# The gate's second half as a second pair of column blocks with two groups of seven products

## The chip, the cores and the metric

The kernel runs on one core of a Trainium2 chip. The metric is the device time of one execution in microseconds; the times of three runs are given as their median. In the profile PE is TensorE (PEld its weight load), DVE VectorE, ACT ScalarE, POOL GpSimd and SP SyncE, which here only issues transfers.

## The reference

One layer of an encoder on 256 rows of 2048 numbers in float32. The change lies in its last step, the per-layer embedding:

```python
gate = jax.nn.sigmoid(rms_norm(x, ple_norm[i]) @ w_ple_gate[i])   # 2048 x 2048
e = (p[i] @ w_ple_proj[i]) * gate                                 # 256 x 2048
x = x + rms_norm(e, ple_post_norm[i])
```

## The kernel before, in words

**Products.** Every float32 matrix product is made of three: a factor is split into a rounded part (`hi`, a cast on ACT, line 181) and the rest (`lo`, a subtraction on DVE, line 184), and PE sums hi x hi (line 323), lo x hi (324) and hi x lo (328). A weight block is loaded as `raw`, four tiles of 128 x 512 (1024 KB), and split in two halves of 128 x 1024 elements. The split weights stand in `whi`/`wlo` (four buffers), and in a phase with groups of seven also in `shi`/`slo` (three). `raw` has five buffers, two of which hold the rows of x to the end, so that three are left for weights; a load is issued when the reads of the buffer's earlier content are done.

**Rows and columns.** The 256 rows are two row tiles t (0 and 1) of 128. The gate's 2048 columns are four column blocks of 512, n = 0 to 3; its 2048 inner terms are four blocks kb = 0 to 3.

**Groups of seven.** `Seven` works on a pair of column blocks. `chunk(kb)` replaces the eight block products (two row tiles, two column blocks, two halves of kb) by seven, in the manner of Strassen and Winograd. The four weight halves b11, b21 (first column block) and b12, b22 (second) give the sums t1 = b11 + b12, t2 = t1 + b22, t4 = t2 + b21 on DVE (line 511), and a DMA issued by POOL adds b22 onto b12. The seven products, in the order 1, 5, 6, 4, 2, 3, 7 (lines 504, 505, 507), take b11, t1, t2, t4, b21, b22 and the accumulated b12, and each of these is split first. On the other side stand sums of the normed rows: `whole_rows` and `sum_forms` (lines 444, 461 and a split). Each product z has a bank of PSUM: 1, 2, 4 and 5 one `acc` each, 6 and 7 one `aux` together, 3 and 8 the other. There are four `acc` and two `aux`, which are given out again in the order in which they come free. Inner blocks outside a group go through `column(side, kbs)`, plain products into the banks 2, 4 or 3, 8.

**The end of the kernel.** The pair n = 0, 1 has one group (kb = 1); `opened` and `gated` combine the banks into the gates, with sigmoids. Then come the projections of p (two inner tiles, one 512 KB load each) for n = 0 and 1, the gate block n = 2 as plain products (`gemm_block`), its projection, and the last column block n = 3 by `gemm_resident`: its weights are split once and kept, row tile 0 runs through all of them, then its projection, then row tile 1, with its projection in two halves. `ple` multiplies projection and gate (line 1570), squares (1571) and applies the gain (1572). When row tile 0 has all its squares, a root and `add` (line 1637) give its output rows, and SP writes them; row tile 1 follows and ends the kernel.

**The order.** Each engine works through its queue in order. PE's order is that of the code; the order on DVE and ACT is set by a scheduler when the program is built, except that `pin` keeps an instruction in its place. `put_off` and `step` place work between the products.

Of the kernel before, what the change touches and what calls it, by code (L numbers as in the profile page):

```python
# [13 lines left out]
ALU = mybir.AluOpType  # L14
# [19 lines left out]
def layer_kernel(ctx: ExitStack, tc: tile.TileContext, a: dict, shapes: dict, out: bass.AP):  # L34
# [35 lines left out]
    def com(tag):  # L70
        return get(comp, tag, *{"sg": (1024, 1), "h": (1024, 2), "sq": (NB, 1), "mid": (2048, 1)}[tag])
# [10 lines left out]
    def small(n=8):  # L82
        return smp.tile([P, 8], F32, tag="sm", name=uid("sm"))[:, :n]
# [1492 lines left out]
    def sigmoid(sg, t, ps):  # L1576
        return nc.scalar.activation(sg[:, t * NB : (t + 1) * NB], ps, AF.Sigmoid, scale=npl.rs(t))

    def gate_block(ps):
        gate = com("h")  # L1580
        for t in range(TT):
            sigmoid(gate, t, ps[t])
        return gate
# [15 lines left out]
    def crossed(s):  # L1599
        v = g1.rearrange("p (t n) -> p t n", t=TT)  # L1600
# [4 lines left out]
    def gated(s):  # L1605
        for t, (ps, other) in enumerate(((s.bank(2), h0[0]), (s.bank(4), h1[1]))):
            nc.vector.tensor_tensor(out=h0[t], in0=ps, in1=other, op=ALU.add)
            sigmoid(g0, t, h0[t])
        crossed(s)

    with sums_phase("sums3") as sevens:
        forms = {1: sum_forms(sevens, whole_rows(sevens, npl(1)), "h")}
        s = Seven(npl, forms.get, ((wg, 0), (wg, NB)), sevens, sevens)
        s.column(0, (0,))
        s.column(1, (0,))
        s.chunk(1, shared)
        put_off(0, opened, s)
        s.column(0, (2,))
        s.column(1, (2,))
        s.column(0, (3,), True)  # L1620
        put_off(0, gated, s)
        s.column(1, (3,), True)
        nc.vector.tensor_tensor(out=g1, in0=s.banks[3.8], in1=g1, op=ALU.add)
        for t in range(TT):
            sigmoid(g1, t, h1[t])
# [5 lines left out]
    gate = com("h")  # L1631
# [11 lines left out]
    s = small(1)  # L1643
    nc.vector.tensor_reduce(out=s, in_=ss[t], axis=AX.X, op=ALU.add)
    r = rsqrt_mean(s, D, 1)
# [142 lines left out]
```

## Time and profile before

| | |
|---|---|
| median of 3 runs | 1818.25 us (1817.67 to 1818.35) |
| profiled execution, from its first to its last instruction | 1817.3 us |
| PE, busy | 1808.1 us, 99% |
| DVE, busy | 1573.3 us, 87% |
| ACT, busy | 1061.1 us, 58% |
| granted PE clock | 1.000 |

A time of the profiled execution besides its span is not given; the median of the runs lies 0.95 us above the span. Busy time is the time in which an engine executes; on PE the ends of products are modelled. The chain that ended last follows the work back from the last instruction, and names what carried it. Rows of the timeline give start, duration, engine, line, operation, what is written from what, and in brackets how long the engine had stood and for what.

### The profile page before, as it was taken

The page shows a single profiled execution, that of the slowest core. Times are in us where ns is not written, and L with a number is a line of the kernel's source. Part 1 is how long each engine was busy: PE and PEld are TensorE (multiplying, and loading weights), DVE is VectorE, ACT ScalarE, POOL GpSimd, SP SyncE. Part 2 cuts the span into 40 slices and gives each one's busy share as a digit, 9 for nine tenths or more (in the row PEclk, how much of TensorE's full clock was granted, in tenths as well). Part 3 has the DMA queues.
Part 4 walks back from the last instruction along what each step waited for, and adds up shares of the span by engine and source line. Part 5 has one row for each costly group of instructions (what it writes and reads, how often), then busy time and mean ns, then how long its engine had stood idle before and what let it go on. Part 6 is the DMA issues. An engine that isn't in the chain of part 4 may idle for free.

```text
span 1817.3 us, 24219 instructions
## 1 busy us (share of the span) xinstructions
PE 1808.1 (99%) x8918; PEld 1496.5 (82%) x8918; DVE 1573.3 (87%) x1839; ACT 1061.1 (58%) x1240; POOL 106.3 (6%) x162
## 2 busy tenths in 40 slices
PE   9999999999999999999999999999999999999998
PEld 7888888888888888888898888888888888888887
DVE  8978889999998896687567899999999999889875
ACT  7444456556565565465685566555565556566664
POOL 0020100000000001110021000000000010000000
PEclk9999999999999999999999999999999999999999
DMA  8899877787877668675646787888777796766673
GB/s 323 266 288 310 262 222 232 233 261 228 261 252 235 186 221 260 195 254 164 219 133 228 221 298 224 258 256 256 235 231 233 236 282 230 235 207 221 203 243 128
DMA packets 235271, 428.41 MB, mean 236 GB/s; under 512 B 24368, under 2 KB 48336, under 8 KB 234992
## 3 DMA queue, kind: packets, MB, share of 16 engines
q1 hardware_dynamic: 223872, 390.06, 65.1%
q0 software_dynamic: 10560, 35.40, 8.9%
q8 instruction: 70, 1.15, 0.3%
q10 hardware_dynamic: 720, 1.41, 0.2%
q14 instruction: 49, 0.40, 0.1%
HBM read 372.41 MB, written 10.88 MB: 211 GB/s over the span
## 4 chain that ended last, share of the span: by engine, by line
PE 95%; DVE 2%; DMA 1%; issue 1%; ACT 1%; SPq 0%; DVEq 0%; ACTq 0%
PE acc L323 16%; PE acc L324 16%; PE acc L328 16%; PE aux L328 7%; PE aux L323 7%; PE aux L324 7%; PE acc L507 5%; PE acc L504 5%; PE acc L505 5%; PE aux L507 3%; PE aux L504 3%; PE aux L505 3%; DVE wlo L184 1%; PE aux L1210 0%; PE acc L1466 0%
## 5 line engine op out<-in xcount | busy, mean ns | idle before, releaser
L184 DVE TENSOR_TENSOR wlo<-raw,whi 128x1024 fp32r<-128x1024 f32 x480 | 580.4, 1222 | 120.7 <-ACT whi L181 120.2
L181 ACT CAST whi<-raw 128x1024 fp32r<-128x1024 f32 x480 | 497.2, 1050 | 286.4 <-PE acc L324 160.9
L323 PE MATMUL acc<-whi,nhi 128*128 128x512 f32 x908 | 356.5, 393 | 1.3 <-ACT whi L274 0.7
L324 PE MATMUL acc<-whi,nlo 128*128 128x512 f32 x908 | 353.7, 390 | 0.0
L328 PE MATMUL acc<-wlo,nhi 128*128 128x512 f32 x908 | 252.4, 389 | 0.0
L184 DVE TENSOR_TENSOR slo<-raw,shi 128x1024 fp32r<-128x1024 f32 x186 | 226.1, 1216 | 15.2 <-ACT shi L181 14.2
L181 ACT CAST shi<-raw 128x1024 fp32r<-128x1024 f32 x186 | 194.9, 1048 | 59.5 <-DMA raw<-in_ffn_w_down 26.1
L323 PEld LDWEIGHTS acc<-whi,nhi 128*128 128x128 f32 x908 | 170.5, 188 | 38.9 <-ACT whi L274 1.7
L328 PEld LDWEIGHTS acc<-wlo,nhi 128*128 128x128 f32 x908 | 170.4, 188 | 35.8 <-DVE wlo L184 0.4
L324 PEld LDWEIGHTS acc<-whi,nlo 128*128 128x128 f32 x908 | 170.5, 188 | 34.6 <-DVE nlo L275 0.3
L181 ACT CAST whi<-sum 128x1024 fp32r<-128x1024 f32 x79 | 83.2, 1054 | 163.7 <-DVE sum L511 152.8
L181 ACT CAST shi<-sum 128x1024 fp32r<-128x1024 f32 x59 | 62.2, 1054 | 106.8 <-DVE sum L511 98.8
L511 DVE TENSOR_TENSOR sum<-sum,raw 128x1024 f32<-128x1024 f32 x92 | 112.1, 1219 | 1.0
L184 DVE TENSOR_TENSOR wlo<-sum,whi 128x1024 fp32r<-128x1024 f32 x79 | 96.2, 1220 | 5.9 <-ACT whi L181 5.3
L574 POOL DMA_DIRECT2D raw<-raw x44 | 38.1, 866 | 1037.6 <-DVE sum L511 634.6
L323 PE MATMUL aux<-whi,nhi 128*128 128x512 f32 x220 | 85.6, 389 | 0.0
L324 PE MATMUL aux<-whi,nlo 128*128 128x512 f32 x220 | 85.6, 389 | 0.0
L184 DVE TENSOR_TENSOR slo<-sum,shi 128x1024 fp32r<-128x1024 f32 x59 | 72.0, 1220 | 1.1 <-ACT shi L181 0.5
L328 PE MATMUL aux<-wlo,nhi 128*128 128x512 f32 x220 | 67.8, 389 | 0.0
L511 DVE TENSOR_TENSOR sum<-raw,raw 128x1024 f32<-128x1024 f32 x46 | 56.1, 1219 | 13.1 <-DMA raw<-in_ffn_w_up 6.3
L323 PE MATMUL acc<-whi,hhi 128*128 128x512 f32 x156 | 60.7, 389 | 0.0
L324 PE MATMUL acc<-whi,hlo 128*128 128x512 f32 x156 | 60.7, 389 | 0.0
(390 smaller groups left out, 3405.5 us busy)
## 6 DMA issues: line engine op xcount, KB each, us to landing
raw<-in_ffn_w_up SPq DMA_DIRECT2D x88, 1024.0 KB, 6.1
raw<-in_ffn_w_down SPq DMA_DIRECT2D x88, 1024.0 KB, 5.3
raw<-in_ffn_w_gate SPq DMA_DIRECT2D x86, 1024.0 KB, 8.0
raw<-in_w_in SPq DMA_DIRECT2D x32, 1024.0 KB, 5.9
raw<-raw POOLq DMA_DIRECT2D x46, 512.0 KB, 5.6
raw<-in_w_out SPq DMA_DIRECT2D x16, 1024.0 KB, 5.4
raw<-in_w_ple_gate SPq DMA_DIRECT2D x16, 1024.0 KB, 5.8
hT<-mid SPq DMA_DIRECT2D x160, 64.0 KB, 4.8
```

Source lines behind the costliest of these rows:

```text
L181: copy = nc.scalar.copy(hi, src)
L184: rest = nc.vector.tensor_tensor(out=lo, in0=src, in1=hi.bitcast(F32), op=ALU.subtract)
L323: nc.tensor.matmul(ps[t], lhsT=lh, rhs=hi[:, j, cols], start=start and j == 0, stop=False)
L324: nc.tensor.matmul(ps[t], lhsT=ll, rhs=hi[:, j, cols], start=False, stop=False)
L328: nc.tensor.matmul(ps[t], lhsT=lh, rhs=lo[:, j, cols], start=False, stop=stop and j == 1)
L504: nc.tensor.matmul(ps, lhsT=lh[j], rhs=hi[:, j], start=begin and j == 0, stop=False)
L505: nc.tensor.matmul(ps, lhsT=ll[j], rhs=hi[:, j], start=False, stop=False)
L507: nc.tensor.matmul(ps, lhsT=lh[j], rhs=lo[:, j], start=False, stop=z in final and j == 1)
L511: nc.vector.tensor_tensor(out=t, in0=x, in1=y, op=ALU.add)
L574: nc.gpsimd.dma_start(b12, b22, accum_op=ALU.add)
```

## The change

The column blocks n = 2 and 3 become a second `Seven` in the same phase. It begins with `chunk(1)` in new banks, then `column(0, (0, 3))`, then `chunk(2)`; the sum forms of kb = 2 are made on the way (`second_form`, ahead of the last column of the first pair). `opened` and `gated` take the pair as an argument. The projections for n = 0, 1, 2 follow. What the last column block still needs, kb = 0 and 3, is `last`: four split halves that stay resident. `last_gate(t)` adds them into bank 3 or 8, sums with what the pair gave on DVE (line 1647 of the changed kernel) and takes the sigmoid; the projection of n = 3 stays as it was, and row tile 1 follows row tile 0.

```diff
-    g0, g1 = es[2:]
-    h0, h1 = ([g[:, t * NB : (t + 1) * NB] for t in range(TT)] for g in (g0, g1))
+    gates = es[2:]
+    def columns(pair):
+        return ([g[:, t * NB : (t + 1) * NB] for t in range(TT)] for g in gates[2 * pair : 2 * pair + 2])
-    def opened(s):
+    def opened(s, pair):
+        h0, h1 = columns(pair)
         nc.scalar.copy(h0[0], s.bank(1))
         nc.vector.tensor_tensor(out=h1[0], in0=s.bank(6), in1=h0[0], op=ALU.add)          # L1593 after
         nc.vector.tensor_tensor(out=h1[1], in0=s.bank(7), in1=h1[0], op=ALU.add)          # L1594
...
+    def gated(s, pair):
+        h0, h1 = columns(pair)
+        v = gates[2 * pair + 1].rearrange("p (t n) -> p t n", t=TT)
+        nc.vector.tensor_tensor(out=h0[0], in0=s.bank(2), in1=h0[0], op=ALU.add)          # L1599
+        nc.vector.tensor_tensor(out=h0[1], in0=s.bank(4), in1=h1[1], op=ALU.add)          # L1600
+        for t in range(TT):
+            sigmoid(gates[2 * pair], t, h0[t])
         nc.vector.tensor_tensor(                                                          # L1603
             out=v, in0=s.bank(5).unsqueeze(1).to_broadcast([P, TT, NB]), in1=v, op=ALU.subtract
         )
...
         s.column(1, (2,))
+        put_off(0, second_form)
         s.column(0, (3,), True)
...
+        s = Seven(npl, forms.get, ((wg, 2 * NB), (wg, 3 * NB)), sevens, sevens)
+        gates += [com("h"), com("h")]
+        s.chunk(1)
+        s.column(0, (0, 3))
+        s.chunk(2, (*shared, 2, 4))
+        opened(s, 1)
+        gated(s, 1)
     own = ctx.enter_context(phase("own"))
-    proj_block(0, g0)
-    proj_block(1, g1)
-    proj_block(2, gate_block(gemm_block(npl, wg, 2 * NB, KD)))
+    for n in range(ND - 1):
+        proj_block(n, gates[n])
+    gate = gates[n + 1]
     n = ND - 1
-    gate = com("h")
-    gates = gemm_resident(npl, a["w_ple_gate"][0], n * NB, KD, own, KD - 8)
+    last = [(npl(kb), half) for kb in (0, 3) for half in weight_halves(wg, 4 * kb, 4, n * NB, own=own)]
     projs = gemm_resident(lambda k: pT, a["w_ple_proj"][0], n * NB, PD // P, own, PD // P, 2)
+    def last_gate(t):
+        z = (3, 8)[t]
+        for part, half in last:
+            gemm_half({t: s.bank(z)}, (part, half), (t,), s.begin(z), half is last[-1][1])
+        g = gate[:, t * NB : (t + 1) * NB]
+        pin(nc.vector.tensor_tensor(out=g, in0=s.bank(z), in1=g, op=ALU.add))             # L1647
+        pin(sigmoid(gate, t, g))
...
     t = 0
-    sigmoid(gate, t, next(gates))
+    last_gate(t)
     ple(n, t, gate, next(projs))
...
     t = 1
-    pin(sigmoid(gate, t, next(gates)))
+    last_gate(t)
```

The names in the rows below carry the number of the buffer's use: `raw_15295` is one load, `wlo_15298` the rest of its weights, `acc_15237` one use of a bank. DVE around the first projection, before: the sums of the first pair (L1607, L1601, L1623), with rests of the gate block n = 2 between them, and `ple` of the projection.

```order
L184 TENSOR_TENSOR wlo_14985<-raw_14982,whi_14984 128x1024
L184 TENSOR_TENSOR wlo_15013<-raw_15010,whi_15012 128x1024
L1607 TENSOR_TENSOR e_2710_14592<-acc_14618,e_2710_14592 128x512
L1607 TENSOR_TENSOR e_2710_14592<-acc_14625,e_2711_14593 128x512
L1601 TENSOR_TENSOR e_2711_14593<-acc_14735,e_2711_14593 128x1024
L184 TENSOR_TENSOR wlo_15041<-raw_15038,whi_15040 128x1024
L1623 TENSOR_TENSOR e_2711_14593<-aux_14661,e_2711_14593 128x1024
L184 TENSOR_TENSOR wlo_15045<-raw_15038,whi_15044 128x1024
L1570 TENSOR_TENSOR e_2710_14592<-acc_14980,e_2710_14592 128x512
L1570 TENSOR_TENSOR e_2710_14592<-acc_14981,e_2710_14592 128x512
```

DVE at the same place after: `raw_15146` is the second load of the group kb = 2, `raw_15239`, `raw_15267` and `raw_15295` are the weights of the projections n = 0, 1 and 2.

```order
L184 TENSOR_TENSOR wlo_15216<-raw_15146,whi_15215 128x1024
L184 TENSOR_TENSOR wlo_15242<-raw_15239,whi_15241 128x1024
L184 TENSOR_TENSOR wlo_15270<-raw_15267,whi_15269 128x1024
L184 TENSOR_TENSOR wlo_15298<-raw_15295,whi_15297 128x1024
L1593 TENSOR_TENSOR h_14988<-aux_15024,h_14987 128x512
L1570 TENSOR_TENSOR e_2710_14592<-acc_15237,e_2710_14592 128x512
L1594 TENSOR_TENSOR h_14988<-aux_15024,h_14988 128x512
L1599 TENSOR_TENSOR h_14987<-acc_15048,h_14987 128x512
L1600 TENSOR_TENSOR h_14987<-acc_15037,h_14988 128x512
L1572 TENSOR_TENSOR e_2708_14590<-e_2710_14592,pg_14587 128x512
L1603 TENSOR_TENSOR h_14988<-acc_15011,h_14988 128x1024
L1570 TENSOR_TENSOR e_2710_14592<-acc_15238,e_2710_14592 128x512
```

The rests of all three projections have moved ahead of the pair's combining and of the first `ple`. The load of `raw_15295` takes the buffer of `raw_15146`. PE's product into `acc_15238`, the bank of the first projection's second row tile, waits for the first L1570, whose `acc_15237` lies in the same bank; before, the product into `acc_14981` waits for the first L1607.

DVE at the end of row tile 0, before: the four adds of row tile 0, two small operations, and the product of row tile 1's gate and projection.

```order
L1646 TENSOR_SCALAR sm_15317<-sm_15317 128x1
L1637 SCALAR_TENSOR_TENSOR x_12725<-e_2708_14590,sm_15317,x_12725 128x512
L1637 SCALAR_TENSOR_TENSOR x_12725<-e_2709_14591,sm_15317,x_12725 128x512
L1637 SCALAR_TENSOR_TENSOR x_12725<-e_2710_14592,sm_15317,x_12725 128x512
L1637 SCALAR_TENSOR_TENSOR x_12725<-e_2711_14593,sm_15317,x_12725 128x512
L1656 TENSOR_REDUCE sm_15386<-sm_14589 128x1
L1657 TENSOR_SCALAR sm_15386<-sm_15386 128x1
L1666 TENSOR_TENSOR h_15205<-acc_15394,h_15205 128x256
```

After, the same place; L1652 is what was L1637, L1681 what was L1666:

```order
L1661 TENSOR_SCALAR sm_15388<-sm_15388 128x1
L1652 SCALAR_TENSOR_TENSOR x_12725<-e_2708_14590,sm_15388,x_12725 128x512
L1652 SCALAR_TENSOR_TENSOR x_12725<-e_2709_14591,sm_15388,x_12725 128x512
L1652 SCALAR_TENSOR_TENSOR x_12725<-e_2710_14592,sm_15388,x_12725 128x512
L1652 SCALAR_TENSOR_TENSOR x_12725<-e_2711_14593,sm_15388,x_12725 128x512
L1647 TENSOR_TENSOR h_14988<-aux_15059,h_14988 128x512
L1671 TENSOR_REDUCE sm_15433<-sm_14589 128x1
L1672 TENSOR_SCALAR sm_15433<-sm_15433 128x1
L1681 TENSOR_TENSOR h_14988<-acc_15441,h_14988 128x256
```

The addition that completes row tile 1's gate (L1647) is new and stands behind the four adds of row tile 0; before, the sigmoid read PE's bank itself.

More of the change, by code (lines that the diff above doesn't have):

```diff
@@ L1577, in sigmoid @@
         return nc.scalar.activation(sg[:, t * NB : (t + 1) * NB], ps, AF.Sigmoid, scale=npl.rs(t))
-    def gate_block(ps):
-        gate = com("h")
-        for t in range(TT):
-            sigmoid(gate, t, ps[t])
-        return gate
     def proj_block(n, gate):
@@ L1597, in opened @@
         nc.vector.tensor_tensor(out=h1[1], in0=s.bank(7), in1=h1[0], op=ALU.add)
-    def crossed(s):
-        v = g1.rearrange("p (t n) -> p t n", t=TT)
+    def gated(s, pair):
[5 more added lines that the diff above has]
+            sigmoid(gates[2 * pair], t, h0[t])
         nc.vector.tensor_tensor(
@@ L1603, in crossed, with second_form @@
         )
[L1605 to L1609, printed above, removed]
     with sums_phase("sums3") as sevens:
         forms = {1: sum_forms(sevens, whole_rows(sevens, npl(1)), "h")}
+        def second_form():
+            forms[2] = sum_forms(sevens, whole_rows(sevens, npl(2)), "h")
         s = Seven(npl, forms.get, ((wg, 0), (wg, NB)), sevens, sevens)
@@ L1640, in layer_kernel @@
     t = 0
-    sigmoid(gate, t, next(gates))
+    last_gate(t)
     ple(n, t, gate, next(projs))
-    s = small(1)
-    nc.vector.tensor_reduce(out=s, in_=ss[t], axis=AX.X, op=ALU.add)
-    r = rsqrt_mean(s, D, 1)
+    total = small(1)
+    nc.vector.tensor_reduce(out=total, in_=ss[t], axis=AX.X, op=ALU.add)
+    r = rsqrt_mean(total, D, 1)
     nc.vector.tensor_scalar(r, r, -2.0, None, op0=ALU.mult)
```

9 lines of the change are left out of this document (4 added, 5 removed).

## The prediction

> **What bounds the kernel now.** I read the page first: the busy rows and the chain that ended last.
>
> ```profile
> PE 1808.1 (99%) x8918; PEld 1496.5 (82%) x8918; DVE 1573.3 (87%) x1839; ACT 1061.1 (58%) x1240; POOL 106.3 (6%) x162
> ...
> PE 95%; DVE 2%; DMA 1%; issue 1%; ACT 1%; SPq 0%; DVEq 0%; ACTq 0%
> ```
>
> PE carries 95% of the chain, so a product taken away is worth its pitch, as long as the weights are split in time. VectorE (DVE) is second with 87%. Next the stages that change: the busy time by window, then the rows of each engine in order of time.
>
> ```profile
> core 0: us, PE busy (x) PEld busy (x) DVE busy (x) ACT busy (x) POOL busy (x), PEclk, DMA share, GB/s
> 1740.00:1800.00 60.00, 60.00 (x266) 49.60 (x265) 40.25 (x50) 33.86 (x46) 0.00 (x0) 1.00 0.51 173
> ...
> 1753.30 0.39 PE L323 MATMUL acc<-whi,pT 128*128 128x512 f32 x1
> 1753.53 0.39 PE L324 MATMUL acc<-whi,pT 128*128 128x512 f32 x1
> ...
> 1755.28 0.91 PE acc L328 x4
> 1758.00 0.91 PE acc L328 x4
> ```
>
> PE never pauses there, and DVE has 60.00 - 40.25 = 19.75 us free. The two rows of the chain lie twelve products apart: 2.72 us, so 0.2267 us a product. At 1753.30 PE turns from the first pair to the first projection; up to there the change leaves its order alone. I go on from that instant, on the clock of this execution.
>
> **The products.** Two groups of seven replace eight block products each: 12 products fewer, 12 x 0.2267 = 2.72 us.
>
> **What the groups ask of DVE.**
>
> ```profile
> 1726.03 1.22 DVE L184 TENSOR_TENSOR slo<-raw,shi 128x1024 fp32r<-128x1024 f32 x1
> 1727.17 1.22 DVE L184 TENSOR_TENSOR wlo<-raw,whi 128x1024 fp32r<-128x1024 f32 x1
> ...
> 1719.39 1.22 DVE L511 TENSOR_TENSOR sum<-sum,raw 128x1024 f32<-128x1024 f32 x1
> ...
> 1709.60 0.76 DVE L461 TENSOR_TENSOR rows<-whole 128x256 f32<-128x256 f32 x2
> ...
> 1756.00 1.29 DVE L1570 TENSOR_TENSOR e<-acc,e 128x512 f32<-128x512 f32 x2
> 1757.20 1.28 DVE L1572 TENSOR_TENSOR e<-e,pg 128x512 f32<-128x512 f32 x2
> ...
> 1721.65 1.05 ACT L181 CAST whi<-raw 128x1024 fp32r<-128x1024 f32 x1
> 1722.60 1.05 ACT L181 CAST shi<-sum 128x1024 fp32r<-128x1024 f32 x1
> ...
> L574 POOL DMA_DIRECT2D raw<-raw x44 | 38.1, 866 | 1037.6 <-DVE sum L511 634.6
> ```
>
> A 1024-wide rest or sum costs DVE a pitch of 1.14 us, a 512-wide operation 0.60, a 256-wide one 0.36 (between its 0.34 and the 0.38 of half the row), a cast on ScalarE (ACT) 0.95. A group needs 7 rests and 3 sums, 11.4 us, while PE works 42 x 0.2267 = 9.5; the two column blocks that it replaces needed 4 rests, 4.6 us. Twice that is +13.6 us. The sum forms of block 2 (two 1024-wide operations, four of 256) are +3.7; the five combining operations of the second pair +3.5; the last gate's two additions +1.2. That is 22 us more where 19.75 are free: DVE, not PE, becomes the bound, and the order on DVE decides. ACT gets seven casts more, 6.7 us, and is busy for 33.86 of the 60 us, so it covers them; SP issues as many loads as before; POOL issues two accumulating DMAs of 0.87 us each with nothing queued behind them. I cost these three at nothing.
>
> **Where DVE's work meets a load.** A weight load is issued when the last rest has read its buffer.
>
> ```profile
> 1736.82 1.22 DVE L184 TENSOR_TENSOR slo<-raw,shi 128x1024 fp32r<-128x1024 f32 x1
> 1739.49 1.22 DVE L184 TENSOR_TENSOR slo<-raw,shi 128x1024 fp32r<-128x1024 f32 x1
> ...
> 1738.07 0.37 SPq L313 DMA_DIRECT2D raw<-in_w_ple_proj  x1
> 1740.74 0.37 SPq L313 DMA_DIRECT2D raw<-in_w_ple_proj  x1
> ...
> raw<-in_w_ple_gate SPq DMA_DIRECT2D x12, 1024.0 KB, 5.7
> raw<-in_w_ple_proj SPq DMA_DIRECT2D x4, 512.0 KB, 3.8
> ...
> DMA to landing us min/median/max: 3.7/5.3/8.1
> ```
>
> The rest of 1736.82 ends at 1738.04 and the load follows at 1738.07; so too 1740.71 and 1740.74. Weights have three buffers here. The same two instants now issue the two loads of the first group, at 5.7 us for 1024 KB; the second lands at 1746.4. The steps, in DVE's order:
>
> 1. From 1746.8 (the rest of the first block precedes) to the last rest of column block 0's second half: 14 operations of 1024 and 2 of 512, 15.9 + 1.2, with 0.1 of waits: it ends at 1764.1. PE's groups in this stretch have their weights just in time; two of the margins are under 0.4 us. I cost that at nothing, since DVE stays the later one.
> 2. That rest frees the buffer of the second load of group two: issued 1764.1, landed 1769.8.
> 3. Nine operations of 1024 (three sums and the rests of blocks two to seven), 10.2 us and 0.4 of waits for casts: the seventh rest ends at 1780.4. The accumulating DMA, issued from POOL behind the first sum (1771.1), is in by 1776.7 at the 5.6 us of its row below, ahead of its cast at 1777.7.
> 4. That rest frees the buffer of the third projection's weights: 3.8 us, landed 1784.2; cast 1.05; DVE's rest, which stands in its queue ahead of all of the pair's combining, ends its pitch at 1786.5.
> 5. Then L1593 (0.60) and the first L1570 (0.69): 1787.8. Only this L1570 gives back the bank into which PE writes the first projection's second row tile. Without a wait PE would write it at 1753.30 + 138 x 0.2267 + 0.1 = 1784.7: PE stands 3.1 us.
>
> ```profile
> raw<-raw POOLq DMA_DIRECT2D x46, 512.0 KB, 5.6
> ```
>
> 6. From there to the rest of the last projection DVE has 14 operations of 512 and 6 of 1024, 15.2 us, and 0.6 of waits: 1803.5. PE waits for rests of the last gate column twice, 1.1 and 0.4 us. The first row tile's gate ends at 1803.55. Unhindered it would end at 1753.30 + 200.1 x 0.2267 + 0.17 (a product runs on past its pitch) = 1798.84; the waits add 3.1 + 1.1 + 0.4 + 0.1 = 4.7 us.
>
> **The end, row tile by row tile.**
>
> ```profile
> 1793.68 0.61 PE L328 MATMUL acc<-wlo,nhi 128*128 128x512 f32 x2
> ...
> 1794.33 0.69 ACT L1577 ACTIVATE h<-acc,sm 128x512 f32<-128x512 f32 x1 [6.61 <-PE acc L328]
> 1795.76 0.69 DVE L1570 TENSOR_TENSOR h<-acc,h 128x512 f32<-128x512 f32 x1 [6.02 <-PE acc L328]
> 1797.23 1.28 ACT L204 ACT_TABLE_LOAD   x1
> 1799.91 2.74 DVE L1637 SCALAR_TENSOR_TENSOR x<-e,sm,x 128x512 f32<-128x512 f32 x4
> ...
> 1806.57 0.69 ACT L1577 ACTIVATE h<-acc,sm 128x512 f32<-128x512 f32 x1 [6.54 <-PE acc L328]
> 1807.35 0.42 DVE L1666 TENSOR_TENSOR h<-acc,h 128x256 f32<-128x256 f32 x1 [4.45 <-ACT h L1577]
> ```
>
> Before, tile 0's work from L1570 (1795.76) to the end of its four adds (1802.65) takes 6.9 us and lies under the 48 products of tile 1's gate. Now tile 1's gate is 24 products, 5.4 us, and on DVE its addition (L1647) stands behind tile 0's adds. From the end of tile 0's gate: addition 0.73, sigmoid 0.76 (each with its hand-over of 0.04), 6.9 to the end of the adds (the next operation enters 0.05 earlier), addition 0.73, sigmoid 0.76, and 0.1 of hand-overs: 10.0 us to tile 1's product with the projection (L1681, L1666 before). 1803.55 + 10.0 = 1813.56, where before it stood at 1807.35: +6.2 us. Before, the same stretch took 1807.35 - 1794.29 = 13.1 us, of which PE's 24 products and a shorter projection are the saving already counted. What follows has the same instructions, 9.95 us to the span's end of 1817.3.
>
> Sum: -2.7 (products) + 4.7 (waits) + 4.2 (the end: 10.0 without waits would give 1808.85, +1.5 against before, and the 2.7 that PE had saved is lost in it) = +6.2 us. The span becomes 1823.5. The three runs' median, 1818.25, is 0.95 above the profiled span; with that kept, 1824.5.
>
> **The bounds.** Two loads lie on the path (steps 1 and 2), two more of 512 KB follow. With the shortest landing of the rows, 3.7, for all, the loads of 1024 KB give 2 x 2.0 back, but the PE saving limits what is left: no less than the end alone, +1.5. With 8.1 for both, 2 x 2.4 = +4.8. I take the median, the value for twelve such loads in this stretch. Beyond that, 0.2 us for each of the two tight margins of step 1.
>
> The clock:
>
> ```profile
> 1812.00:1815.00 3.00, 0.43 (x2) 0.00 (x0) 0.93 (x2) 0.58 (x1) 0.00 (x0) 1.00 0.87 312
> 1815.00:1817.30 2.30, 0.00 (x0) 0.00 (x0) 0.00 (x0) 0.00 (x0) 0.00 (x0) 0.98 0.13 49
> ...
> 1811.31 1.13 PE L1693 MATMUL aux<-e,diag 128*128 128x512 f32 x2 [0.19 <-ACT diag L1692]
> ```
>
> The last product ended at 1812.44, the granted clock stayed 1.00 up to 1815 and was 0.98 after: at least 2.6 us of idling cost nothing. The waits of 3.1 and, between the warming products and the last one, of 4.2 us (1813.3 to 1817.5) lie just beyond what these rows cover. I take no loss. The Trainium skill ("TensorE: Matmul & The Clock Gate", Part 1) says that the clock falls to half after an idle window of about 3.4 us that runs freely. By it the 3.1 us would pass, and the 4.2 us might slow the last products by up to their own length; the trace's 2.6 us at full clock agree with it and reach no further.
>
> **Rivals.** The yardstick: 0.2%, 3.6 us, is about what a measurement of this kernel can tell from no change.
>
> - *Only the end costs.* If DVE keeps ahead (loads of 3.7 us, sums that fit the 19.75 us), the bank is free in time, and +1.5 us remain: 1819.7. For it: the 22 us are near the free time. Against it: step 4 is a chain of a load, a cast, a rest and two operations, 7.4 us, against 4.3 us from the seventh rest to PE's need.
> - *Not slower: PE remains the bound.* The place is L1647 of tile 1. If tile 0's adds were over when tile 1's gate ends, only one addition more would stand on the path: -2.72 + 0.73 = -2.0, 1816.3. It decides from the point where tile 0's 8.4 us (0.73 + 0.76 + 6.9) fit into PE's 5.4 + 0.7 (two remaining pairs of the projection); they don't, by 2.3 us, and the order is fixed.
> - *Slow loads.* Both loads of the path at 8.1: 1829.3. Group two's come within 5 us of each other and of another; the maximum stands in the rows, at a time when two ran together.
> - *The clock falls.* The two last products take twice their 1.13 us, and if PE's wait grows past 4 us, some 3.4 us after it run at half: +1.1 to +2.8, about 1826.5. The skill's rule cited above is of this kind.
>
> **How the numbers follow.** Forecast, DVE and the bank bind: 0.62, with 1822.5 to 1827 as its own range. Only the end: 0.13. PE remains the bound: 0.05. Slow loads: 0.15. Clock: 0.05. Slower than 1821.9 (0.2%): 0.62 + 0.15 + 0.05 = 0.82. Within 0.2%: the end alone and most of the PE case, 0.16. Faster by more, below 1814.6: 0.02, as even the 2.72 us whole would not reach it. For 8 in 10 I leave out the PE case, half of the end-only case and half of the slow loads: 1820 to 1828.5.
>
> **What would show it.** In the profile after: PE waiting about 3 us at the second row tile of the first projection, for DVE's L1570; DVE without gaps from there to the last projection's rest; waits of PE for rests of the last gate column; L1647 of tile 1 right behind four L1652; PE idle in the last 8 us. Wrong would make it: a DVE that is done with the seventh rest before 1778, a bank given back by another instruction, loads far off 5.7 us.

## The result: half a per cent slower, by the mechanism forecast and by more than its size

The changed kernel takes 1828.26 us (median of 4 runs, 1827.24 to 1830.92) against 1818.30 us before (4 runs beside them, 1817.67 to 1820.45). The ratio is 1.0052 with a 95% interval of 1.004 to 1.0065: slower by 10.0 us, where 6.2 were forecast. The profiled execution took 1827.57 us, with a span of 1825.7.

The page of the changed kernel, its busy row and its chain:

```profile
PE 1809.1 (99%) x8906; PEld 1494.9 (82%) x8906; DVE 1595.1 (87%) x1864; ACT 1069.6 (59%) x1248; POOL 109.2 (6%) x164
...
PE 90%; DVE 5%; DMA 2%; issue 2%; ACT 1%; SPq 0%; DVEq 0%; ACTq 0%
```

PE has the 12 products less (8918 to 8906), yet its share of the chain falls from 95% to 90%; DVE, loads and "issue" take the rest. In the stage that changed, DVE has filled up, from 40.25 to 51.30 us, and PE shows holes:

```profile
1740.00:1800.00 60.00, 55.89 (x239) 44.89 (x238) 51.30 (x56) 36.20 (x46) 1.75 (x2) 0.97 0.57 185
```

The timeline of the changed kernel along the steps of the prediction (rows of PE, ACT and DVE, in order of time; in brackets the idle time and what ended it):

```profile
1751.82 0.62 PE L328 MATMUL aux<-wlo,nhi 128*128 128x512 f32 x2
...
1761.60 1.22 DVE L184 TENSOR_TENSOR wlo<-raw,whi 128x1024 fp32r<-128x1024 f32 x1
...
1769.95 1.23 DVE L511 TENSOR_TENSOR sum<-raw,raw 128x1024 f32<-128x1024 f32 x1 [1.11 <-DMA raw<-in_w_ple_gate]
...
1779.40 2.35 DVE L184 TENSOR_TENSOR wlo<-raw,whi 128x1024 fp32r<-128x1024 f32 x2
...
1784.84 1.04 ACT L181 CAST whi<-raw 128x1024 fp32r<-128x1024 f32 x1 [1.96 <-DMA raw<-in_w_ple_proj]
...
1785.91 1.23 DVE L184 TENSOR_TENSOR wlo<-raw,whi 128x1024 fp32r<-128x1024 f32 x1 [1.77 <-ACT whi L181]
1787.06 0.68 DVE L1593 TENSOR_TENSOR h<-aux,h 128x512 f32<-128x512 f32 x1
1787.66 0.68 DVE L1570 TENSOR_TENSOR e<-acc,e 128x512 f32<-128x512 f32 x1
...
1788.39 0.50 PE L323 MATMUL acc<-whi,pT 128*128 128x512 f32 x1 [3.80 <-DVE e L1570]
```

The first row is PE's last pair of products in the first pair of column blocks. Its start plus 0.45 us is the instant at which PE turns to what the change reorders: 1752.27 here, 1753.30 before. Over the profiles of this case it moves between 1751.9 and 1754.1 with no change ahead of it in PE's order, so profiles are compared from this turn on. The rest of 1761.60 is step 1's. Of the two rests from 1779.40 the first, up to 1780.62, is the group's seventh. The last rows are the forecast's chain, in its order: the load of the third projection, its cast, the rest, L1593, L1570, and PE, which had stood 3.80 us for that L1570.

| us from the turn | before | forecast | after |
|---|---|---|---|
| last rest of inner block 0 ends (step 1) | | 10.8 | 10.55 |
| second load of group two is in (2) | | 16.5 | 17.7 |
| seventh rest ends (3) | | 27.1 | 28.35 |
| third projection's load is in (4) | | 30.9 | 32.5 |
| PE goes on at the bank (5) | no wait | 34.5 | 36.12 |
| row tile 0's gate is taken up (6) | 41.03 | 50.3 | 53.69 |
| row tile 1's product with the projection | 54.05 | 60.3 | 63.46 |
| end of the span | 64.0 | 70.2 | 73.43 |

Up to the bank the loss against the forecast is 1.6 us. Another 1.8 us arises between bank and gate, where the forecast had DVE busy but for 0.6 us. The windows of the changed kernel show what happened (the third number from the end is the granted PE clock), and below them two rows of PE from the timeline:

```profile
1787.00:1789.00 2.00, 0.61 (x3) 0.51 (x4) 2.00 (x5) 0.00 (x0) 0.00 (x0) 1.00 1.04 386
1789.00:1790.00 1.00, 1.00 (x4) 0.82 (x3) 1.00 (x2) 0.45 (x1) 0.00 (x0) 0.59 1.04 399
1790.00:1791.00 1.00, 1.00 (x4) 0.74 (x3) 1.00 (x3) 1.00 (x2) 0.00 (x0) 0.50 0.61 231
1791.00:1792.00 1.00, 1.00 (x4) 0.81 (x3) 1.00 (x2) 1.00 (x3) 0.00 (x0) 0.50 0.10 39
1792.00:1793.00 1.00, 1.00 (x4) 0.77 (x4) 0.46 (x1) 1.00 (x3) 0.00 (x0) 0.70 0.06 23
...
1790.49 0.63 PE L323 MATMUL acc<-whi,pT 128*128 128x512 f32 x1
1790.92 0.63 PE L324 MATMUL acc<-whi,pT 128*128 128x512 f32 x1
```

PE comes back from its wait at full clock, and 0.8 us later the clock is at half: 0.82 us of the second from 1789, two whole ones and 0.6 of the last, 3.4 us in all. In this spell products start 0.43 us apart instead of 0.23. DVE, which then had nothing to read, stands (0.46 busy from 1792), and a row of the same timeline gives that gap:

```profile
1794.21 0.69 DVE L1570 TENSOR_TENSOR e<-acc,e 128x512 f32<-128x512 f32 x1 [1.75 <-PE acc L328]
```

The end, row tile by row tile, in the timeline of the changed kernel (it answers to the rows of L1577, L1637, L1666 and L1693 of the kernel before in the prediction):

```profile
1805.96 0.69 DVE L1647 TENSOR_TENSOR h<-aux,h 128x512 f32<-128x512 f32 x1 [0.17 <-PE aux L328]
...
1811.60 2.74 DVE L1652 SCALAR_TENSOR_TENSOR x<-e,sm,x 128x512 f32<-128x512 f32 x4
1814.26 0.68 DVE L1647 TENSOR_TENSOR h<-aux,h 128x512 f32<-128x512 f32 x1
...
1815.73 0.42 DVE L1681 TENSOR_TENSOR h<-acc,h 128x256 f32<-128x256 f32 x1 [0.54 <-ACT h L1577]
...
1819.66 1.88 PE L1708 MATMUL aux<-e,diag 128*128 128x512 f32 x2 [3.79 <-ACT diag L1707]
```

Row tile 1's L1647 stands right behind the four adds; from the first L1647 to L1681 it is 9.77 us. The last two products take 1.88 us, where they took 1.13.

### The profile page after: what moved, and what is told of

It is laid out like the page before. It is cut to its first block, busy times and chain, and to the rows that moved or that the text cites. A ratio compares the mean times of both kernels' runs of the same rounds, so it can differ in the third digit from the quotient of the medians.

```text
span 1825.7 us, 24254 instructions
## 1 busy us (share of the span) xinstructions
PE 1809.1 (99%) x8906; PEld 1494.9 (82%) x8906; DVE 1595.1 (87%) x1864; ACT 1069.6 (59%) x1248; POOL 109.2 (6%) x164
## 4 chain that ended last, share of the span: by engine, by line
PE 90%; DVE 5%; DMA 2%; issue 2%; ACT 1%; SPq 0%; DVEq 0%; ACTq 0%
PE acc L323 15%; PE acc L324 15%; PE acc L328 15%; PE aux L328 7%; PE aux L323 7%; PE aux L324 7%; PE acc L504 4%; PE acc L505 4%; PE acc L507 4%; PE aux L507 3%; PE aux L504 3%; PE aux L505 3%; DVE wlo L184 1%; DMA raw<-in_ffn_w_down 1%; DVE sum L511 1%
## 5 line engine op out<-in xcount | busy, mean ns | idle before, releaser
L184 DVE TENSOR_TENSOR wlo<-raw,whi 128x1024 fp32r<-128x1024 f32 x474 | 573.2, 1222 | 114.7 <-ACT whi L181 114.3
L323 PE MATMUL acc<-whi,nhi 128*128 128x512 f32 x852 | 334.7, 393 | 1.4 <-ACT whi L274 0.8
L324 PE MATMUL acc<-whi,nlo 128*128 128x512 f32 x852 | 332.0, 390 | 0.0
L184 DVE TENSOR_TENSOR slo<-raw,shi 128x1024 fp32r<-128x1024 f32 x192 | 233.3, 1215 | 16.0 <-ACT shi L181 15.8
L181 ACT CAST shi<-raw 128x1024 fp32r<-128x1024 f32 x192 | 201.3, 1049 | 63.7 <-DMA raw<-in_ffn_w_down 23.0
L328 PE MATMUL acc<-wlo,nhi 128*128 128x512 f32 x852 | 236.5, 389 | 0.0
L323 PEld LDWEIGHTS acc<-whi,nhi 128*128 128x128 f32 x852 | 159.9, 188 | 37.1 <-ACT whi L274 1.8
L328 PEld LDWEIGHTS acc<-wlo,nhi 128*128 128x128 f32 x852 | 159.8, 188 | 33.8 <-DVE wlo L184 0.5
L324 PEld LDWEIGHTS acc<-whi,nlo 128*128 128x128 f32 x852 | 160.0, 188 | 32.5 <-DVE nlo L275 0.2
L323 PE MATMUL aux<-whi,nhi 128*128 128x512 f32 x236 | 91.9, 390 | 0.0
```

The lines of the kernel that those rows point to most:

```text
L181: copy = nc.scalar.copy(hi, src)
L184: rest = nc.vector.tensor_tensor(out=lo, in0=src, in1=hi.bitcast(F32), op=ALU.subtract)
L323: nc.tensor.matmul(ps[t], lhsT=lh, rhs=hi[:, j, cols], start=start and j == 0, stop=False)
L324: nc.tensor.matmul(ps[t], lhsT=ll, rhs=hi[:, j, cols], start=False, stop=False)
L328: nc.tensor.matmul(ps[t], lhsT=lh, rhs=lo[:, j, cols], start=False, stop=stop and j == 1)
```

## Experiments

The change had four suspects: VectorE's sum of work, its order at the bank, the clock, and the end. All times are medians of 4 to 11 runs beside runs of the kernel before on the same chip. Those have medians of 1818.85 to 1819.4 beside the experiments and 1818.30 beside the changed kernel, so its loss is 9 to 10 us. Runs of one kernel spread over 1.5 to 6 us (8 once), so small differences are read from the turn in the profiles; the last three columns are us from it. Even so two profiles of the same code can lie a microsecond apart: e2_warm is the changed kernel up to its last products, and its gate comes at 54.70 instead of 53.69 (why is said under the clock).

| kernel | us | ratio to before, 95% | gate of tile 0 | product of tile 1 | end |
|---|---|---|---|---|---|
| changed | 1828.26 | 1.0052 (1.004 to 1.0065) | 53.69 | 63.46 | 73.43 |
| e1_order | 1829.64 | 1.0053 (1.0041 to 1.0066) | 54.81 | 64.58 | 74.69 |
| e7_bank | 1824.26 | 1.0032 (1.002 to 1.0044) | 49.90 | 59.68 | 69.46 |
| e11_plain | 1828.35 | 1.0047 (1.0034 to 1.0059) | 53.17 | 62.94 | 72.75 |
| e10_filled | 1826.95 | 1.0041 (1.0027 to 1.0055) | 51.70 | 61.47 | 71.57 |
| e3_repeat | 1827.85 | 1.005 (1.0037 to 1.0064) | 52.70 | 62.47 | 72.52 |
| e12_noform | 1823.53 | 1.0028 (1.0019 to 1.0036) | 49.28 | 59.05 | 69.11 |
| e6_tail | 1821.36 | 1.0011 (1.0002 to 1.0019) | 46.52 | 56.28 | 66.15 |
| e2_warm | 1829.49 | 1.0053 (1.0041 to 1.0066) | 54.70 | 64.48 | 74.33 |
| e8_split_adds | 1824.27 | 1.0029 (1.0018 to 1.0039) | 49.88 | 59.03 | 68.79 |
| e4_one | 1821.26 | 1.0013 (1.0004 to 1.0022) | 46.73 | 56.50 | 66.32 |
| e5_one_long | 1819.67 | 1.0003 (0.9994 to 1.0012) | 43.39 | 54.11 | 64.00 |
| e9_long_bank | 1823.22 | 1.0022 (1.0013 to 1.0031) | 47.35 | 58.35 | 68.22 |

### The order on VectorE, moved too far

```diff
-    for n in range(ND - 1):
+    for n in range(ND - 2):
         proj_block(n, gates[n])
+    with tc.issue_after(crossed.ins):        # L1603 of the second pair
+        proj_block(n + 1, gates[n + 1])
```

> The changed kernel with one move: the third projection's split and products come behind the last combining operation of the second pair (L1603) on VectorE, and nothing else differs. Theory (the bank of the first projection waits because VectorE stands at the rest of the third projection, behind a load of 3.8 us, ahead of the combining): TensorE's wait at the second row tile of the first projection falls from 3.8 us to under 1 us, the clock stays full at 1789 us, the gate of row tile 0 ends 3 to 5 us earlier, and the time is 1823.3 to 1825.3 us, 3 to 5 less than the changed kernel's 1828.26. Rival (VectorE's sum of work is the bound, whatever its order): the wait turns up again at the rests behind it, and the time falls by less than 1 us, to 1827.3 or more.

The wait did fall, and nothing was won. PE's rows in the timeline of e1_order, and below them SP's issue of the last projection's load, ACT's last operations up to the cast of it, and a window in which the DMA moves nothing any more (the last number, GB/s):

```profile
1786.46 0.50 PE L323 MATMUL acc<-whi,pT 128*128 128x512 f32 x1 [1.00 <-DVE h L1599]
...
1799.32 0.79 PE L323 MATMUL acc<-whi,pT 128*128 128x512 f32 x1 [4.82 <-ACT whi L181]
```

```profile
1791.09 0.37 SPq L313 DMA_DIRECT2D raw<-in_w_ple_proj  x1
...
1796.86 0.63 ACT L1571 ACTIVATE sq<-e 128x512 f32<-128x512 f32 x1
...
1797.61 0.63 ACT L1571 ACTIVATE sq<-e 128x512 f32<-128x512 f32 x1
...
1798.24 1.03 ACT L181 CAST whi<-raw 128x1024 fp32r<-128x1024 f32 x1
...
1795.00:1796.00 1.00, 0.00 (x0) 0.00 (x0) 0.86 (x2) 1.00 (x4) 0.00 (x0) 1.00 0.00 0
```

The rest that I moved back reads the `raw` buffer into which the last projection is loaded. In the changed kernel that load is issued at 1787.17, 34.9 us from the turn; here at 37.6 us. But it takes 3.7 us here and 6.3 there, where the loads of the last gate column still run beside it, so it is in at 41.3 us here and at 41.2 there. PE stands 4.82 us for the cast, and the cast stands in ACT's queue: from 1790.61 on ACT works without a gap, with four casts of the last gate column, two sigmoids and four squares, and comes to this cast 3.4 us after the load is in. PE, which had passed the bank 3.2 us sooner, comes back from that wait at half clock. The rival was right in its time and named the wrong place: the wait turned up at ACT's cast, not at DVE's rests. Neither theory had followed ACT. Whether another order there would have kept the gain was not tried.

### The order, moved only as far as the idle time goes

```diff
         s.chunk(2, (*shared, 2, 4))
+        weights = [proj_weights(0), proj_weights(1)]
+        freeing = proj_block(0, gates[0], weights[0])[0]     # its first L1570
+        with tc.issue_after(freeing.ins):
+            weights.append(proj_weights(2))
         opened(s, 1)
```

> The changed kernel with the order of VectorE alone moved, otherwise than before: two combining operations (L1593, L1594 of the second pair) and the product that gives back the bank (L1570 of the first projection's row tile 0) stand ahead of the third projection's rest, in time that VectorE had idle (1.77 us), so that the rest itself, and the load of the last projection that waits for its buffer, come no later than in the changed kernel. Theory (the changed kernel loses its time at the bank and to the halved clock behind that wait; the move of the whole combining failed because it delayed the rest and with it the last projection's load): TensorE's wait falls from 3.8 to about 1.4 us, the clock stays 1.00 there, no wait for the last projection's cast, and the time is 3 to 4 us below the changed kernel's 1828.3: 1824.3 to 1825.3. Rival (VectorE's sum of work decides): TensorE waits as much later, at the rests of the last gate column, and the time falls by less than 1 us: 1827.3 or more.

DVE in e7_bank does L1596 and L1597 (L1593 and L1594 of the changed kernel) and L1570 in the time in which it had waited for the cast, and the third projection's rest follows, at 33.47 us from the turn, where it was at 33.64:

```profile
1784.05 0.68 DVE L1596 TENSOR_TENSOR h<-aux,h 128x512 f32<-128x512 f32 x1
1784.77 0.69 DVE L1597 TENSOR_TENSOR h<-aux,h 128x512 f32<-128x512 f32 x1
...
1786.41 1.23 DVE L184 TENSOR_TENSOR wlo<-raw,whi 128x1024 fp32r<-128x1024 f32 x1 [0.36 <-ACT whi L181]
```

```profile
1786.11 0.50 PE L323 MATMUL acc<-shi,pT 128*128 128x512 f32 x1 [1.22 <-DVE e L1570]
...
1788.99 0.47 PE L323 MATMUL acc<-whi,pT 128*128 128x512 f32 x1 [1.22 <-DVE e L1570]
```

PE's wait of 3.80 has become two of 1.22 (a second one at the next bank, which I had not expected), the clock is 1.00 from 1786 to 1794, and the time is 4.0 us less, at the edge of the 3 to 4 expected. So the order at the bank held 4 us. The run prices the new order as a whole: the split weights of the first projection lie in other buffers (`shi`), and the scheduler has placed one rest of the last gate column sooner (1790.99, where the changed kernel has it at 1799.42). e11_plain below has these buffers with the old order at the bank, and waits there as before. On ACT the cast of the last projection now comes right behind those of the gate column (three from 1793.65), ahead of the four squares that stood in its way in e1_order.

### The clock behind the wait

e3_repeat put 12 more products into the wait:

```diff
-        ps = gemm_block(lambda k: pT, a["w_ple_proj"][0], n * NB, PD // P)
+        ps = [acc(), acc()]                                  # n = 0 alone
+        for half in list(weight_halves(a["w_ple_proj"][0], 0, PD // P, 0)):
+            for t in (0, 0, 0, 1):
+                gemm_half(ps, (pT, half), (t,), True, True)
```

> The changed kernel, in which the six products of the first projection's row tile 0 are done three times over (each time afresh into the same bank, so the value is the same): 12 products, 2.72 us, of extra work on TensorE right ahead of its wait of 3.8 us. Theory (the wait costs twice, as a wait for VectorE, and by halving the clock for 3.3 us behind it): TensorE does 2.7 us more and idles 1.1 us there; the clock is 1.00 at 1789 to 1793; the first product behind the wait starts at the same 1788.4, since VectorE sets it, and the time falls by 1 to 1.6 us, to 1826.7 to 1827.3. Rival (the slow products behind the wait cost nothing on the path): 1828.3. Rival (TensorE's time is what counts): 12 products more, 1831.

From the turn the gate of row tile 0 comes 1.0 us sooner, at full clock and with 12 products more; the medians (0.4 us apart) don't tell it. But the scheduler had also put DVE's operations in another order, and the wait had become two (1.82 and 1.52 us), so this run alone proves nothing. The pair e11_plain and e10_filled fixes DVE's order by hand; the second operation of `opened` and all of `gated` stand behind the first L1570 in both, and only e10_filled has the repeated products.

> The changed kernel, with VectorE's order around the bank fixed by hand as it was found there (three rests of projections, L1593, the product L1570 that gives back the bank, then the rest of the combining); it is the base for the next two. Expected as the changed kernel: 1828.3 within 1 us, TensorE's wait at the bank 3.8 us within 0.5, the clock at half for about 3 us behind it.

> The base (VectorE's, ScalarE's and the queues' order the same) with the six products of the first projection's row tile 0 done three times over: 12 products of 0.2267 us, 2.7 us, inside TensorE's wait. Theory (the clock falls behind a wait of 3.8 us and not behind one of about 1.1 us, and the slow products are on the path): clock 1.00 throughout 1787 to 1795, and the gate of row tile 0 ends 1 to 1.6 us sooner than in the base, counted from TensorE's turn to the second pair; the time is 1 to 1.6 us less, with 12 products more. Rival (VectorE sets the pace behind the bank too, and the slow products are covered): the same as the base within 0.4 us. Rival (12 products cost their time): 2.7 us more.

PE's row behind the wait in e11_plain, and its windows:

```profile
1788.13 0.50 PE L323 MATMUL acc<-shi,pT 128*128 128x512 f32 x1 [3.49 <-DVE e L1570]
```

```profile
1789.00:1790.00 1.00, 0.91 (x4) 0.32 (x3) 0.93 (x3) 0.39 (x1) 0.00 (x0) 0.76 1.07 410
1790.00:1791.00 1.00, 0.98 (x2) 0.83 (x3) 1.00 (x2) 1.00 (x2) 0.00 (x0) 0.50 0.59 225
1791.00:1792.00 1.00, 1.00 (x4) 0.79 (x3) 1.00 (x3) 1.00 (x4) 0.00 (x0) 0.50 0.09 35
1792.00:1793.00 1.00, 1.00 (x4) 0.81 (x3) 0.97 (x1) 1.00 (x2) 0.00 (x0) 0.53 0.06 23
```

The same two views of e10_filled:

```profile
1789.70 0.50 PE L323 MATMUL acc<-shi,pT 128*128 128x512 f32 x1 [1.07 <-DVE e L1570]
```

```profile
1789.00:1791.00 2.00, 1.30 (x6) 1.05 (x6) 2.00 (x5) 0.90 (x3) 0.00 (x0) 1.00 1.05 408
1791.00:1793.00 2.00, 1.77 (x8) 1.23 (x7) 2.00 (x4) 2.00 (x4) 0.00 (x0) 1.00 0.79 300
```

With PE busy in its wait the clock stays, and the gate of row tile 0 comes 1.47 us sooner (53.17 to 51.70). The medians differ by 1.4 us with 2.7 us more work on PE, but the runs overlap (1826.21 to 1828.62 and 1826.03 to 1827.50). From PE's return at the bank to the gate it is 17.39 us in e11_plain and 16.03 in e10_filled; e12_noform below, with the same order and full clock, has 16.16. So a spell of 3.4 us at half clock costs some 1.2 to 1.5 us here.

The price is not fixed. In e2_warm the clock falls ahead of PE's return (0.59 in the window from 1788; PE is back at 1789.78 after a wait of 4.11) and stays at half up to 1795, 6.8 us in all. The same stretch takes 18.39 us there and 17.57 in the changed kernel, with the same code.

### VectorE's sum of work

e12_noform is e11_plain without the sum forms of block 2; the second group multiplies those of block 1 again.

```diff
         def second_form():
-            forms[2] = sum_forms(sevens, whole_rows(sevens, npl(2)), "h")
+            forms[2] = forms[1]
```

> The base without the sum forms of block 2: the second group multiplies block 1's forms again (so its output isn't the reference's), and VectorE is spared six operations, 2 x 1.14 + 4 x 0.36 = 3.7 us, ahead of the second pair; TensorE's products and the loads are the same in number. Theory (VectorE's sum of work ahead of the bank is what is late, and the loads follow it, because each is issued when VectorE has read a buffer): all instants from the second group's load on come up to 3.7 us sooner, the wait at the bank is 0.1 to 1 us instead of 3.8, the clock stays full, and the time is 4 to 5.3 us less than the base: 1823 to 1824.3. Rival (the chain of load, cast and rest at the third projection sets the wait, whatever VectorE has to do ahead): wait over 3 us, and less than 1 us won.

```profile
1784.73 1.23 DVE L184 TENSOR_TENSOR wlo<-raw,whi 128x1024 fp32r<-128x1024 f32 x1 [1.93 <-ACT whi L181]
...
1787.21 0.50 PE L323 MATMUL acc<-shi,pT 128*128 128x512 f32 x1 [1.67 <-DVE e L1570]
```

3.7 us of DVE's work taken away ahead of the pair take 4.8 us off the median, as expected (3.6 from the turn in the profiles), and the clock stays full; by the stretch from bank to gate above, that is some 1.2 us of the 4.8. The size at the place itself was not as expected: the third projection's rest (turn at 1754.09) comes at 30.6 us instead of 33.3, so 2.7 of the 3.7 us arrive there, and PE still waits 1.67 us; the load and the cast ahead of that rest keep DVE waiting 1.93. Sum and order act on one path: with less work DVE frees the buffers sooner, with another order it frees the bank sooner.

### The end

e6_tail is the kernel before with the end alone. Its core:

```diff
+    for kb in (1, 2):
+        for half in list(weight_halves(wg, 4 * kb, 4, n * NB)):
+            gemm_half(ps, (npl(kb), half), range(TT), kb + half[0] == 1, kb + half[0] == 3)
+    for t in range(TT):
+        nc.scalar.copy(gate[:, t * NB : (t + 1) * NB], ps[t])
+    last = [(npl(kb), half) for kb in (0, 3) for half in weight_halves(wg, 4 * kb, 4, n * NB, own=own)]
...
-    sigmoid(gate, t, next(gates))
+    last_gate(t)
```

> The kernel before with the end alone: the last gate column's blocks 1 and 2 are multiplied for both row tiles first and copied aside, and blocks 0 and 3 close it row tile by row tile, with VectorE's addition ahead of the sigmoid; no group of seven products more, and as many products as before. My working (row tile 1's addition stands behind the four adds of row tile 0): the gate of row tile 0 ends 24 products later, 1794.29 + 5.44 = 1799.73, and row tile 1's product with the projection comes 10.0 us later, 1809.7 where it was 1807.35: +2.3 us, 1820.6. Rival (the addition costs only itself): +0.7 us, 1819.0. Rival (VectorE and ScalarE have the time, TensorE alone counts): 0, 1818.3.

```profile
1804.00 2.74 DVE L1643 SCALAR_TENSOR_TENSOR x<-e,sm,x 128x512 f32<-128x512 f32 x4
1806.66 0.68 DVE L1651 TENSOR_TENSOR h<-acc,h 128x512 f32<-128x512 f32 x1
...
1808.13 0.42 DVE L1680 TENSOR_TENSOR h<-acc,h 128x256 f32<-128x256 f32 x1 [0.54 <-ACT h L1577]
```

Row tile 1's addition stands behind the adds, its product comes 2.2 us later than before (turn at 1751.85: 56.28 against 54.05) and the end 2.15; 2.3 were worked out. The median is 2.5 us higher, the ratio's interval 0.4 to 3.5 us.

e2_warm asks what the slow last products cost: `range(22)` for `range(10)` at the warming products.

> The changed kernel with 22 instead of 10 warming products ahead of the last two, 12 x 0.2267 = 2.7 us of TensorE's idle 3.8 us at the end. Theory (an idle window of 3.8 us halves the clock): the two last products take 1.13 us again instead of 1.88, and the time falls by 0.75 us to about 1827.5. Rival (the last products are long for another reason): they keep 1.88 us, and the time stays at 1828.3; a third possibility, that the longer warming block comes in the way of the last products, would give 1828.5 or more.

PE's row of the last two products in e2_warm:

```profile
1821.91 1.12 PE L1708 MATMUL aux<-e,diag 128*128 128x512 f32 x2 [1.09 <-ACT diag L1707]
```

A window of the last transfers, in e2_warm and then in the changed kernel (the last number is GB/s, the third from the end the clock):

```profile
1823.00:1824.00 1.00, 0.03 (x1) 0.00 (x0) 0.53 (x1) 0.59 (x1) 0.00 (x0) 1.00 0.94 348
```

```profile
1821.00:1822.00 1.00, 0.54 (x1) 0.00 (x0) 0.29 (x1) 0.42 (x1) 0.00 (x0) 0.50 1.02 377
```

The products are back at 1.12 us at full clock, so the idling was what slowed them. Nothing came of it: from tile 1's product (1817.95) to the end it is 9.85 us, 9.97 in the changed kernel and 9.95 before. In all three the output goes out at some 340 to 380 GB/s for two to three microseconds; I take it that this queue of transfers covers the products, but that the transfers set the end was not tried by itself.

e8_split_adds takes e7_bank and puts two of row tile 0's adds behind row tile 1's addition.

```diff
-    for n_ in range(ND):
+    for n_ in range(2):
         add(t, n_, r)
+    joined = last_gate(1)
+    with tc.issue_after(joined.ins):
+        for n_ in range(2, ND):
+            add(t, n_, r)
```

> The kernel with the bank's product ahead of the third projection's rest (1824.26), and at the end only two of row tile 0's four adds stand ahead of row tile 1's addition, the other two behind it, under ScalarE's sigmoid. Theory (row tile 1's addition waits behind the four adds, 2.7 us): it enters 1.3 us sooner, the product with the projection 0.6 to 0.8 us sooner (the other two adds end then), and the time is about 0.7 less: 1823.5. Rival (TensorE's gate of row tile 1 ends just there): nothing won, 1824.3. Rival (the outputs' transfers set the end): the product comes sooner and the span's end does not.

```profile
1808.93 1.41 DVE L1660 SCALAR_TENSOR_TENSOR x<-e,sm,x 128x512 f32<-128x512 f32 x2
1810.26 0.68 DVE L1654 TENSOR_TENSOR h<-aux,h 128x512 f32<-128x512 f32 x1
1810.86 1.41 DVE L1660 SCALAR_TENSOR_TENSOR x<-e,sm,x 128x512 f32<-128x512 f32 x2
```

The product comes 0.65 us sooner from the turn (59.68 to 59.03; from the gate it is 9.15 us instead of 9.78) and the end 0.67: the addition does wait for the adds. The medians are the same (1824.26 and 1824.27); 0.7 us is below what they tell.

### One group instead of two

All three kernels here leave out `second_form`, which one group does not need. e4_one keeps the new end; e5_one_long has 36 products a row tile there; e9_long_bank is that with e7_bank's move.

```diff
         s = Seven(npl, forms.get, ((wg, 2 * NB), (wg, 3 * NB)), sevens, sevens)
         gates += [com("h"), com("h")]
-        s.chunk(1)
-        s.column(0, (0, 3))
-        s.chunk(2, (*shared, 2, 4))
-        opened(s, 1)
+        s.chunk(1, shared)
+        put_off(0, opened, s, 1)
+        s.column(1, (2,))                    # e4_one alone
+        s.column(0, (0, 2, 3), True)
...
-    last = ... for kb in (0, 3)
+    last = ... for kb in (0, 2, 3)           # e5_one_long, e9_long_bank
```

> The changed kernel with one group of seven (block 1) instead of two; block 2 of the last two gate columns goes by ordinary products ahead, and the end (blocks 0 and 3 row tile by row tile) is kept. Six products more, but VectorE has one group (6.8 us) and the sum forms of block 2 (3.7 us) less. Theory (the groups cost by VectorE's 22 us against 19.75 free, and the end costs its own part): without the 10.5 us VectorE keeps ahead, TensorE never waits for a bank, and what is left is the end: against before the gate of row tile 0 ends 18 products later (+4.1), row tile 1's product follows at 10.0 instead of 13.1 us (-3.1), so 1 to 1.4 us over before's 1818.9: 1820. Rival (the groups' waits come from loads and not from VectorE's sum): one group waits too, with half the loss, 1823 or more. Rival (only TensorE counts): 6 products fewer than before, 1817.5.

> One group of seven (block 1), and the last gate column keeps blocks 0, 2 and 3, 36 products a row tile, for the end. Theory (row tile 0's 8.4 us of VectorE and ScalarE must fit under row tile 1's products, here 36 x 0.2267 + 0.7 = 8.9 us; and VectorE keeps ahead with one group): six products fewer than before, one addition of 0.73 more on the path, -0.6 us against before: 1818.3, and TensorE has no wait over 0.5 us. Rival (VectorE's order still holds a bank or a load, with one group too): 1 to 3 us more than before, 1820 to 1822.

> The kernel with one group and 36 products a row tile at the end, in which VectorE does the first projection's products and the second pair's combining ahead of the third projection's rest. Theory (with one group the order no longer matters, since VectorE is ahead): within 0.5 us of the same kernel without the move, about 1818.3. Rival (the order still holds a bank there): whatever that kernel waits at the bank is won here, and it comes out 1 to 3 us below it.

With one group PE has no gap at the bank in e4_one, and 0.24 us in e5_one_long. e4_one is 2.3 us over before from the turn, where 1.0 to 1.4 were expected: PE's order takes four products of the last projection for row tile 0 and six of half the width for row tile 1 ahead of the end of row tile 0's gate, 1.6 us that I had not counted (46.73 instead of 45.1). Its tail is the 9.77 us of the changed kernel. e5_one_long ends where the kernel before ends, 64.00 us from the turn, with a ratio of 1.0003 (0.9994 to 1.0012): six products are saved and an addition and small waits spend them; the 0.6 us expected did not come. e9_long_bank was the theory's miss: the move that won 4 us above loses 3.6 here (4.2 from the turn). The scheduler then put all rests of the last gate column behind the projections' operations, where e5_one_long has one of them ahead, at 1780.66:

```profile
1790.36 6.90 DVE L184 TENSOR_TENSOR wlo<-raw,whi 128x1024 fp32r<-128x1024 f32 x6
...
1791.63 0.73 PE L328 MATMUL aux<-wlo,nhi 128*128 128x512 f32 x2 [3.08 <-DVE wlo L184]
```

PE stands 3.08 us for a rest, and the clock drops behind that too. No kernel run beats the one before; e5_one_long is as fast.

## Why the prediction was right, and where it was too small

- *DVE becomes the bound*: right in the main. DVE's busy time in the stage grew by 11 us within the same window, and e12_noform, with 3.7 us less of it, won 4.8. But between turn and bank DVE itself stood 6.5 us for casts and loads: the path runs through DVE and the loads by turns, as the steps have it, and the sum of 22 us against 19.75 free ones is not by itself what sets the time.
- *Steps 1 to 3*: the order was right; the loads were slow. The second load of group two landed some 7.1 us after its issue at 1762.8, between the 5.7 taken and the 8.1 named as the bound: 1.2 us late. The third projection's took 4.1 instead of 3.8 us.
- *Steps 4 and 5*: right in every link. PE goes on at 36.12 instead of 34.5 us from the turn; it waits 3.8 instead of 3.1, as the bank came 1.6 us late and PE itself 0.9. e7_bank, with L1570 ahead of the rest, waits 1.22 there.
- *Step 6, and "I take no loss" for the clock*: the step that failed. The wait halved the clock for 3.4 us; e11_plain against e10_filled and e12_noform prices that at 1.2 to 1.5 us of the 1.8 lost between bank and gate; the rest of them stays open. DVE was then not without gaps but stood 1.75 us for PE, so the sentence on DVE there was wrong as well. The rival "the clock falls" had this price (1.1 to 2.8 us) and a chance of 0.05, from a threshold of 4 us that no row supported.
- *The end*: right, 9.77 us where 10.0 were worked out, and e6_tail gives it alone, 2.15 us for 2.3. The two last products did slow, as that rival said, and it cost nothing.
- *The sum*, from the turn: -2.7 for products, +8.1 for waits and clock (53.65 - 45.54) instead of 4.7, +4.0 for the end instead of 4.2: +9.4 instead of +6.2.
- *The 0.95 us between span and time*: mis-sized. It set a median of other runs against one span. The profiled execution of the changed kernel lies 1.87 us above its span, and runs of the kernel before with their spans lie as far above (1818.71 and 1816.8, for one). That is 0.9 us of the 3.8 by which the median missed; 3.2 are the steps above, 0.7 is that the profiled execution lies below the median, and -1.0 that its turn came earlier.
- *Rivals*: "only the end" and "PE remains the bound" are excluded for this kernel; e4_one, without the second group, comes near the first of them (+2.3 us instead of +1.5). "Slow loads" was half so: one load on the path took 7.1 us.

The Trainium skill ("TensorE: Matmul & The Clock Gate", Part 1) has the clock watched by free-running windows of about 3.4 us. The traces agree in the length of the spells at half: 3.42 us (changed kernel, 0.82 + 2 + 0.60), 3.42 (e11_plain) and 3.40 (e9_long_bank), and twice that, 6.8 us, in e1_order and e2_warm. They don't agree with a whole idle window as the condition, by which the prediction let 3.1 us pass: 3.08 us were enough in e9_long_bank.

## What to carry to other kernels

When work moves from the busiest engine to the second, add up the second's free time in that stage first, and then follow each buffer and bank: which instruction gives it back, and what stands ahead of it in its queue. An operation moved forward frees one thing sooner and brings the waiting engine sooner to the next, which must be ready too: in e1_order PE won 3 us at the bank and met a cast that stood far back in ScalarE's queue. In a kernel like this a wait of some 3 us or more on TensorE is to be priced twice, once for itself and once for the clock behind it.

## What the runs showed of the hardware that was not expected

- Waits of 3.08 (e9_long_bank), 3.49 (e11_plain), 3.80 (changed), 4.11 (e2_warm) and 4.82 us (e1_order) brought half clock; waits of 1.00 to 1.82 us did not, and the last products of e6_tail ran at full clock after 2.42 us. The length alone does not say when: at the ends of e4_one and e11_plain the last products came after 3.83 and 4.06 us of idling and ran in 1.12 us at full clock (in e11_plain it fell as they ended, 0.62 in the window from 1820), while 3.79 us in the changed kernel and 3.16 in e8_split_adds were enough to slow them to 1.88 and 1.55.
- The fall can come after the restart: there were 0.8 us of full clock behind the wait in the changed kernel and 1.0 us in e9_long_bank; in e1_order and e2_warm the clock fell before it.
